# Four places for a feed-forward set's first raw quarters, three for other raw weights, and a 4 KB scratch for GpSimd's transfers

## The chip, the core and the metric

The program runs on one core of a Trainium2 chip: TensorE (PE) multiplies, VectorE (DVE), ScalarE (ACT) and GpSimd (POOL) work element by element, SyncE (SP) and GpSimd issue the transfers from device memory. The metric is device microseconds of one execution, from its first to its last instruction and what lies around it; less is better.

## What is computed

Two layers of an encoder trunk over 768 tokens (512 and 256, two groups that share all weights), in float32. Cut to what matters here:

```python
x = x + W_o( g_att * P_att(DiffAttn(n)) + g_rec * P_rec(BiRGLRU(n)) )   # n = RMSNorm(x)
...
h2 = rmsnorm(x, norm2_g)
return x + jnp.square(jax.nn.relu(h2 @ w_ff1)) @ w_ff2      # D_MODEL 1024, D_FF 4096
```

The change touches how the weights of all these products are brought in, above all those of the last line.

## The kernel before

**Precision and products.** Every float32 operand is split into a rounded part `hi` and a remainder `lo`; a product takes three matmuls (hi·hi, hi·lo, lo·hi).

**Feed-forward.** The 4096 hidden columns are worked in 8 pieces of 512 (loop over `c`). A piece has a first stage (`w_ff1`, lines 1028 to 1030) and a second (`w_ff2`, lines 1099 to 1102). Each is a 2x2 block product by Strassen's scheme: 7 products in place of 8, from 4 raw quarters `a1`, `b1`, `b2`, `a2` of the weight block and from sums of them. One set of weights is thus 4 loads of 128x1024 floats and 7 operands: `a1`, `a2`, `b2` as they are, `P1 = b1 + b2`, `P2 = P1 ± a1`, `P3 = a1 ± b1` (written over `b1`), `P4 = a2 ± P2` (written over `P2`). The four sums are DVE instructions of line 250. The second stage takes its products in the order 1, 2, 6, 5, 3, 7, 4 (`FP2`), 24 matmuls each. After each half of a product DVE adds the accumulator into the residual `x` (line 1069, tiles sY or sZ), and the next product may write that accumulator only after this. DVE also forms sums of the hidden blocks (line 1069, tiles e) and their `lo` parts (line 213, tiles sZ or sX; in the first layer sZ): the operands `o2[q]` of the products.

**Weights.** `prefetch` walks a fixed list (`plan`) and prepares up to 8 operands ahead. A sum, and every weight that is no raw quarter, is split by ACT (line 210, `whi`) and DVE (line 213, `wlo`). A raw quarter `a1`, `a2`, `b2` is rounded and negated by ACT (lines 294, 295), and a transfer that GpSimd issues (line 296) adds the raw quarter from device memory into `wlo`. `whi` and `wlo` have 4 places each (`WB`).

**Places.** `a1` and `b1` of a set lie in tiles `rw` with 2 places, `b2` and `a2` in tiles `raw` with 2 places, which all other raw weights use too. SP issues these loads in the order of the program; a load waits until the place it takes is free, and those behind it wait with it.

**Order.** TensorE's order is written by hand. On the other engines a scheduler orders the program by its own estimate of when operands are ready; each engine then works strictly in that order.

Of the kernel before, what the change touches and what calls it, by code (L numbers as in the profile page):

```python
# [9 lines left out]
F32 = mybir.dt.float32  # L10
# [6 lines left out]
P = 128  # L17
# [66 lines left out]
def trunk_kernel(ctx: ExitStack, tc: tile.TileContext, xT, wqk, wv, wx, wy, wg0, wg1, wa, wr, wo, wf1, wf2,  # L84
                 wf2s, rgw, vec, rep, rot, out):
    nc = tc.nc
# [3 lines left out]
    wp = ctx.enter_context(tc.tile_pool(name="wp", bufs=1))  # L90
# [112 lines left out]
    def nm(s):  # L203
        uid[0] += 1
        return f"{s}_{uid[0]}"

    def split(hi, lo, src, eng="act"):

        if eng == "act":
            S.activation(hi, src, AF.Copy)  # L210
        else:
            V.tensor_copy(out=hi, in_=src)
        V.tensor_tensor(out=lo, in0=src, in1=hi.bitcast(F32), op=ALU.subtract)  # L213
# [29 lines left out]
    fw, fpool = {}, [None]  # L243

    def ff_operand(w, l, c, x):

        ep_, sub = fpool[0], w == "wf2"

        def two(out, u, v, op):
            V.tensor_tensor(out=fw[out], in0=fw[u], in1=fw[v], op=op)  # L250

        if x == "a1":
            for i, y in enumerate(("a1", "b1", "b2", "a2")):
                if i < 2:
                    fw[y] = ep_.tile([P, 1024], F32, tag="rw", name=nm("rw"), bufs=2)
                else:
                    fw[y] = wp.tile([P, 1024], F32, tag="raw", name=nm("raw"), bufs=2)
                fw["d" + y] = WT[w][l][c][i]
                nc.sync.dma_start(out=fw[y], in_=fw["d" + y])
            fw["P1"] = fw["P2"] = None  # L260
        if x in ("P1", "P2") and fw["P1"] is None:
            fw["P1"] = ep_.tile([P, 1024], F32, tag="ws", name=nm("ws"), bufs=2)
            two("P1", "b1", "b2", ALU.add)
        if x == "P2":
            fw[x] = ep_.tile([P, 1024], F32, tag="ws", name=nm("ws"), bufs=2)
            two(x, "P1", "a1", ALU.subtract if sub else ALU.add)
        elif x == "P3":
            fw[x] = fw["b1"]
            two(x, "a1", "b1", ALU.subtract if sub else ALU.add)
        elif x == "P4":  # L270
            fw[x] = fw["P2"]
            two(x, "a2", "P2", ALU.subtract if sub else ALU.add)
        return fw[x], fw.get("d" + x)

    def prefetch(upto):
        while len(ready) < min(upto, len(plan)):
            k = plan[len(ready)]
            acc = None
            if k[0] in ("wf1", "wf2"):
                (raw, acc), n = ff_operand(*k), 1024  # L280
            else:
                src = WT[k[0]]
                for x in k[1:]:
                    src = src[x]
                n = src.shape[1]
                raw = wp.tile([P, n], F32, tag="raw", name=nm("raw"), bufs=2)
                nc.sync.dma_start(out=raw, in_=src)
            hi = wp.tile([P, n], F32R, tag="whi", name=nm("whi"), bufs=WB)
            lo = wp.tile([P, n], F32R, tag="wlo", name=nm("wlo"), bufs=WB)
            if acc is None:  # L290
                split(hi, lo, raw)
            else:

                S.activation(hi, raw, AF.Copy)  # L294
                S.activation(lo, hi.bitcast(F32), AF.Copy, scale=-1.0)  # L295
                G.dma_start(out=lo, in_=acc, accum_op=ALU.add)  # L296
            ready.append((hi, lo))

    def wload(*key):
        i = pos[0]  # L300
        pos[0] += 1
        assert plan[i] == key, (plan[i], key)
        prefetch(i + 1 + AHEAD)
        r, ready[i] = ready[i], None
        return r
# [115 lines left out]
    def norm1(l, xt, alloc):  # L421

        nh = [slot(gh, F32R) for k in range(KT)]
        nl = [slot(gl, F32R) for k in range(KT)]
        ss, st_ = [], []

        def sums():
            if not st_:
                st_.append(slots(gx, F32R))
            return st_[0]  # L430

        for g in range(2):
            if g:
                prefetch(4)
            ss.append(squares(xt, g, alloc, sums, lambda k: prep(xt, vt[l][:, V_N1:V_N1 + KT], nh, nl, g, k)))
        return nh, nl, ss
# [6 lines left out]
    for k in range(KT):  # L443
        if k % 4 == 0:
            prefetch(1 + k // 4)
        nc.sync.dma_start(out=xt[k][:, 0:TA], in_=xT[k][:, 0:TA])
# [7 lines left out]
    for l in range(DEPTH):  # L454
# [292 lines left out]
        def chain():  # L747
            for kind, i in FILL:
                yield from (vproj(i, rtok) if kind == "wv" else proj(i, rtok) if kind == "wqk" else gate0(rb))

        n, it = 0, chain()
# [24 lines left out]
        for j in range(KT):  # L776
# [3 lines left out]
            for g in range(2):  # L780
                off, n = GROUPS[g]
# [134 lines left out]
        for j in range(KT):  # L916
# [5 lines left out]
            for g in range(2):  # L922
                off, n = GROUPS[g]
# [54 lines left out]
        for j in range(KT):  # L978
            w1 = wload("wo", l, j)
            for g in range(2):  # L980
                off, n = GROUPS[g]
# [235 lines left out]
```

## Time and profile before

| | |
|---|---|
| runs shown (3) | 2791.74, 2795.38, 2795.95 us; median 2795.38 |
| profiled execution | 2797.47 us, of which the span is 2795.7 |
| mean granted TensorE clock | 0.976 of full |
| busy | PE 2620.9 us, DVE 1987.8, ACT 1582.9, POOL 175.5 |
| moved by transfers | 248.08 MB, mean 89 GB/s |

The two layers have the same stages: attention, its projection, the recurrent branch, the output product, then the feed-forward, whose pieces follow each other some 71 us apart. A timeline row gives start and length of an instruction; what stands in brackets is how long its engine had stood before it, and which instruction ended that. [...]

### The profile page before, as it was taken

To read this page: it belongs to the slowest core of one execution; us is meant where nothing else is said; L and a number is where in the kernel's file an instruction comes from. 1 tells how busy PE (TensorE), PEld (TensorE's weight loads), DVE (VectorE), ACT (ScalarE), POOL (GpSimd) and SP (SyncE) were. 2 spreads that over 40 slices of the span, in tenths; PEclk is the share of its full clock that TensorE was granted. 3 is DMA by queue.
4 is the path that set the end of the run, shared out by engine and by line. 5 is a ranking of instruction groups with operands and counts; after the bars stand their busy time and mean duration, and the time that the engine had idled before them with its cause. 6 is when DMAs were issued, how large, how long until landed. Compare 5 with 4: busy or idle time off the path is not lost.

```text
span 2795.7 us, 40462 instructions
## 1 busy us (share of the span) xinstructions
PE 2620.9 (94%) x16096; PEld 2458.3 (88%) x16096; DVE 1987.8 (71%) x3243; ACT 1582.9 (57%) x2570; POOL 175.5 (6%) x227
## 2 busy tenths in 40 slices
PE   8999999999998888888899999999999988888889
PEld 8999888888888888888899998888888888888889
DVE  8877863798568666666568788637984686666666
ACT  7787861677235444444467878616772354444444
POOL 0000000000200000000100000000003000000000
PEclk9999999999999999999999999999999999999999
DMA  3111123122424444444321111232224144444444
GB/s 127 59 46 56 50 95 106 60 70 95 136 64 106 106 106 106 106 103 101 104 66 59 48 54 50 94 106 64 65 95 143 58 106 106 106 106 105 106 102 110
DMA packets 70877, 248.08 MB, mean 89 GB/s; under 512 B 8992, under 2 KB 12448, under 8 KB 70688
## 3 DMA queue, kind: packets, MB, share of 16 engines
q1 hardware_dynamic: 48384, 161.50, 17.9%
q0 software_dynamic: 21584, 83.37, 13.7%
q8 instruction: 126, 2.06, 0.3%
q10 hardware_dynamic: 720, 0.62, 0.1%
q14 instruction: 63, 0.52, 0.1%
HBM read 226.59 MB, written 18.87 MB: 88 GB/s over the span
## 4 chain that ended last, share of the span: by engine, by line
PE 54%; DVE 19%; issue 17%; DMA 5%; ACT 4%; POOL 1%; DVEq 0%; ACTq 0%; POOLq 0%
PE d L311 6%; PE d L313 6%; PE d L312 6%; PE d L1028 5%; PE d L1029 5%; PE d L1030 5%; DMA rw<-wf 5%; DVE wlo L213 4%; DVE sZ L1069 2%; DVE sY L1069 2%; PE d L474 2%; PE d L473 2%; PE d L472 2%; PE d L336 2%; PE d L335 2%
## 5 line engine op out<-in xcount | busy, mean ns | idle before, releaser
L210 ACT ACTIVATE whi<-raw 128x1024 fp32r<-128x1024 f32 (+1 forms) x180 | 183.4, 1020 | 320.6 <-PE d L312 162.7
L213 DVE TENSOR_TENSOR wlo<-raw,whi 128x1024 fp32r<-128x1024 f32 (+1 forms) x180 | 218.8, 1219 | 44.9 <-ACT whi L210 43.8
L210 ACT ACTIVATE whi<-ws 128x1024 fp32r<-128x1024 f32 x93 | 98.6, 1060 | 167.5 <-DVE ws L250 105.2
L1099 PE MATMUL d<-sX,whi 128*128 128x384 f32 x448 | 157.3, 351 | 34.3 <-DVE sZ L1069 34.3
L1101 PE MATMUL d<-sX,whi 128*128 128x384 f32 x448 | 157.5, 352 | 32.0 <-DVE sX L213 32.0
L1099 PE MATMUL d<-sZ,whi 128*128 128x384 f32 x392 | 138.3, 353 | 33.1 <-DVE sY L1069 33.1
L1101 PE MATMUL d<-sZ,whi 128*128 128x384 f32 x392 | 138.5, 353 | 31.9 <-DVE sZ L213 31.9
L294 ACT ACTIVATE whi<-raw 128x1024 fp32r<-128x1024 f32 x62 | 65.4, 1055 | 178.9 <-PE d L1101 156.2
L1102 PE MATMUL d<-sX,wlo 128*128 128x384 f32 x448 | 156.2, 349 | 0.0
L311 PE MATMUL d<-sZ,whi 128*128 128x512 f32 (+1 forms) x448 | 150.8, 337 | 0.2 <-DVE rec L403 0.2
L312 PE MATMUL d<-sZ,whi 128*128 128x512 f32 (+1 forms) x448 | 150.8, 337 | 0.0
L312 PE MATMUL d<-sX,whi 128*128 128x512 f32 (+1 forms) x448 | 150.8, 336 | 0.0
L313 PE MATMUL d<-sZ,wlo 128*128 128x512 f32 (+1 forms) x448 | 150.6, 336 | 0.0
L296 POOL DMA_DIRECT2D wlo<-wf x93 | 81.2, 874 | 1098.4 <-ACT wlo L295 1046.1
L472 PE MATMUL d<-whi,sY 128*128 128x256 f32 x512 | 147.8, 289 | 0.0
L472 PE MATMUL d<-whi,sZ 128*128 128x256 f32 x512 | 147.4, 288 | 0.0
L201 ACT ACTIVATE p<-s,nb,sc 128x512 f32<-128x512 f32 (+1 forms) x192 | 134.6, 703 | 21.4 <-DVE nb L652 19.7
L474 PE MATMUL d<-whi,sZ 128*128 128x256 f32 x512 | 145.3, 284 | 0.0
L473 PE MATMUL d<-wlo,sY 128*128 128x256 f32 x512 | 145.2, 283 | 0.0
L474 PE MATMUL d<-whi,sX 128*128 128x256 f32 x512 | 144.7, 283 | 0.0
L473 PE MATMUL d<-wlo,sZ 128*128 128x256 f32 x512 | 144.7, 283 | 0.0
L213 DVE TENSOR_TENSOR wlo<-ws,whi 128x1024 fp32r<-128x1024 f32 x93 | 113.4, 1219 | 43.4 <-ACT whi L210 43.3
(388 smaller groups left out, 9093.6 us busy)
## 6 DMA issues: line engine op xcount, KB each, us to landing
wlo<-wf POOLq DMA_DIRECT2D x93, 512.0 KB, 6.9
rw<-wf SPq DMA_DIRECT2D x62, 512.0 KB, 3.9
raw<-wf SPq DMA_DIRECT2D x62, 512.0 KB, 3.6
raw<-wqk SPq DMA_DIRECT2D x32, 512.0 KB, 4.0
raw<-wg SPq DMA_DIRECT2D x32, 512.0 KB, 3.7
raw<-wv SPq DMA_DIRECT2D x16, 512.0 KB, 3.9
raw<-wa SPq DMA_DIRECT2D x16, 512.0 KB, 4.2
raw<-wx SPq DMA_DIRECT2D x16, 512.0 KB, 3.7
```

What stands on the lines that cost most here:

```text
L210: S.activation(hi, src, AF.Copy)
L213: V.tensor_tensor(out=lo, in0=src, in1=hi.bitcast(F32), op=ALU.subtract)
L311: PE.matmul(ps, lhsT=wh, rhs=xh, start=(k == 0), stop=False)
L312: PE.matmul(ps, lhsT=wh, rhs=xl, start=False, stop=False)
L313: PE.matmul(ps, lhsT=wl, rhs=xh, start=False, stop=(k == n - 1))
L472: PE.matmul(j, lhsT=xh, rhs=hi[:, kk], start=(k == 0), stop=False)
L473: PE.matmul(j, lhsT=xh, rhs=lo[:, kk], start=False, stop=False)
L474: PE.matmul(j, lhsT=xl, rhs=hi[:, kk], start=False, stop=(k == 7))
L1028: PE.matmul(ps, lhsT=hi[:, k], rhs=oh, start=new and k == 0, stop=False, skip_group_check=True)
L1099: PE.matmul(ps, lhsT=hi[:, r, k], rhs=oh[:, k], start=q in (1, 2, 7) and k == 0, stop=False, skip_group_check=True)
L1101: PE.matmul(ps, lhsT=hi[:, r, k], rhs=ol[:, k], start=False, stop=False, skip_group_check=True)
L1102: PE.matmul(ps, lhsT=lo[:, r, k], rhs=oh[:, k], start=False, stop=k == 1, skip_group_check=True)
```

## The change

Three numbers: `rw` gets 4 places, `raw` gets 3, and the part of SBUF that is set aside for the transfers issued by GpSimd shrinks from the default (16384 bytes a partition in the built program) to 4096. Three tiles of 4096 bytes take up what that sets free.

```diff
@@ -252,9 +252,9 @@
         if x == "a1":
             for i, y in enumerate(("a1", "b1", "b2", "a2")):
                 if i < 2:
-                    fw[y] = ep_.tile([P, 1024], F32, tag="rw", name=nm("rw"), bufs=2)
+                    fw[y] = ep_.tile([P, 1024], F32, tag="rw", name=nm("rw"), bufs=4)
                 else:
-                    fw[y] = wp.tile([P, 1024], F32, tag="raw", name=nm("raw"), bufs=2)
+                    fw[y] = wp.tile([P, 1024], F32, tag="raw", name=nm("raw"), bufs=3)
@@ -283,7 +283,7 @@
-                raw = wp.tile([P, n], F32, tag="raw", name=nm("raw"), bufs=2)
+                raw = wp.tile([P, n], F32, tag="raw", name=nm("raw"), bufs=3)
                 nc.sync.dma_start(out=raw, in_=src)
@@ -1202,7 +1202,7 @@
-    nc = _bacc.Bacc("TRN2", target_bir_lowering=False, num_devices=1)
+    nc = _bacc.Bacc("TRN2", target_bir_lowering=False, num_devices=1, dynamic_dma_scratch_size=4096)
```

TensorE's and GpSimd's rows are the same in both programs; those of DVE, ACT and SP move. Three places, all in the second stage of piece 2 of the first layer (1010 to 1052 us in the trace of before). In the names, rw_1757, rw_1758, raw_1759 and raw_1760 are a1, b1, b2, a2 of the next set (first stage of piece 3), ws_1767 is its P1 and ws_1774 its P2, later its P4; rw_1791, rw_1792, raw_1793 and ws_1806 are a1, b1, b2 and P1 of the set after that. sY are the residual, sZ_1781 and sZ_1784 the `lo` parts for products 7 and 4.

DVE, from the middle of product 5's additions to product 4's operand, before:

```order
L1069 TENSOR_TENSOR sY_1516_8698<-sY_1516_8698,d_1771_10656 128x2x384
L1069 TENSOR_TENSOR e_1735_10370<-e_1735_10370,e_1732_10367 128x768
L1069 TENSOR_TENSOR sY_1513_8695<-sY_1513_8695,d_1770_10642 128x2x384
L250 TENSOR_TENSOR ws_1767_10636<-rw_1758_10567,raw_1759_10569 128x1024
L1069 TENSOR_TENSOR sY_1515_8697<-sY_1515_8697,d_1771_10656 128x2x384
L250 TENSOR_TENSOR ws_1774_10677<-ws_1767_10636,rw_1757_10565 128x1024
L1069 TENSOR_TENSOR sY_1514_8696<-sY_1514_8696,d_1789_10816 128x2x384
L213 TENSOR_TENSOR wlo_1769_10639<-ws_1767_10636,whi_1768_10638 128x1024
L1069 TENSOR_TENSOR sY_1516_8698<-sY_1516_8698,d_1790_10830 128x2x384
L213 TENSOR_TENSOR wlo_1776_10680<-ws_1774_10677,whi_1775_10679 128x1024
L250 TENSOR_TENSOR rw_1758_10567<-rw_1757_10565,rw_1758_10567 128x1024
L213 TENSOR_TENSOR sZ_1784_10777<-e_1735_10370,sZ_1784_10777 128x768
```

DVE, the same stretch now (product 5's first addition stands just ahead; sZ_1784 is the next row after the last):

```order
L250 TENSOR_TENSOR ws_1767_10636<-rw_1758_10567,raw_1759_10569 128x1024
L1069 TENSOR_TENSOR sY_1516_8698<-sY_1516_8698,d_1771_10656 128x2x384
L250 TENSOR_TENSOR ws_1774_10677<-ws_1767_10636,rw_1757_10565 128x1024
L1069 TENSOR_TENSOR sY_1513_8695<-sY_1513_8695,d_1770_10642 128x2x384
L213 TENSOR_TENSOR sZ_1781_10742<-e_1733_10368,sZ_1781_10742 128x768
L1069 TENSOR_TENSOR sY_1515_8697<-sY_1515_8697,d_1771_10656 128x2x384
L213 TENSOR_TENSOR wlo_1769_10639<-ws_1767_10636,whi_1768_10638 128x1024
L1069 TENSOR_TENSOR e_1735_10370<-e_1735_10370,e_1732_10367 128x768
L1069 TENSOR_TENSOR sY_1514_8696<-sY_1514_8696,d_1789_10816 128x2x384
L250 TENSOR_TENSOR rw_1758_10567<-rw_1757_10565,rw_1758_10567 128x1024
L1069 TENSOR_TENSOR sY_1516_8698<-sY_1516_8698,d_1790_10830 128x2x384
L213 TENSOR_TENSOR wlo_1776_10680<-ws_1774_10677,whi_1775_10679 128x1024
```

Between product 5's first addition and sZ_1784 the same instructions stand in both; the sum ws_1767 has moved ahead of four of them.

DVE, from sZ_1784 to the next first stage, now (before, the two rows that write ws_1806 and rw_1792 stood behind wlo_1786):

```order
L213 TENSOR_TENSOR sZ_1784_10777<-e_1735_10370,sZ_1784_10777 128x768
L250 TENSOR_TENSOR ws_1774_10677<-raw_1760_10571,ws_1774_10677 128x1024
L250 TENSOR_TENSOR ws_1806_10924<-rw_1792_10846,raw_1793_10848 128x1024
L250 TENSOR_TENSOR rw_1792_10846<-rw_1791_10844,rw_1792_10846 128x1024
L1069 TENSOR_TENSOR sY_1514_8696<-sY_1514_8696,d_1789_10816 128x2x384
L1069 TENSOR_TENSOR sY_1516_8698<-sY_1516_8698,d_1790_10830 128x2x384
L213 TENSOR_TENSOR wlo_1783_10748<-rw_1758_10567,whi_1782_10747 128x1024
L213 TENSOR_TENSOR wlo_1786_10782<-ws_1774_10677,whi_1785_10781 128x1024
L250 TENSOR_TENSOR ws_1807_10926<-ws_1806_10924,rw_1791_10844 128x1024
```

Two sums of the set after next now stand ahead of the additions of product 4.

SP, the loads of these sets, now:

```order
L259 DMA rw_1757_10565<-wf1 128x1024
L259 DMA raw_1729_10333<-wf2 128x1024
L259 DMA rw_1758_10567<-wf1 128x1024
L259 DMA raw_1759_10569<-wf1 128x1024
L259 DMA rw_1791_10844<-wf2 128x1024
L259 DMA raw_1760_10571<-wf1 128x1024
L259 DMA raw_1793_10848<-wf2 128x1024
L259 DMA rw_1792_10846<-wf2 128x1024
```

Before, SP issued raw_1729 ahead of rw_1757, then raw_1759, raw_1760, rw_1758, rw_1791, raw_1793, rw_1792: rw_1758 came last of its set. In the built programs rw_1758 takes the place of rw_1727 (P3 of the set in use, read last by wlo_1753) before, and that of the same quarter of the set two before (first stage of piece 2) now; raw_1759 takes the place of raw_1729 before, and that of b2 of the set two before now; raw_1793 now takes that of raw_1728, and rw_1792 that of rw_1727.

## Rows read from the trace of the kernel before

**Rows 1.** Windows: us, busy PE, PEld, DVE, ACT, POOL, granted clock, DMA share, GB/s.

```profile
600.00:800.00 200.00, 199.45 (x1141) 175.13 (x1141) 136.41 (x193) 103.73 (x131) 24.99 (x24) 1.00 0.31 103
...
796.90:868.00 71.10, 71.10 (x413) 66.03 (x412) 55.71 (x87) 43.92 (x70) 4.39 (x5) 1.00 0.35 83
...
1010.10:1081.20 71.10, 61.76 (x338) 60.93 (x337) 48.04 (x56) 32.61 (x41) 5.24 (x6) 0.93 0.45 104
```

**Rows 2.** Waits of PE: total us, times, longest.

```profile
PE d L1099 <- DVE sZ L1069: 34.3, 15, 4.0
PE d L1099 <- DVE sY L1069: 33.1, 14, 3.9
PE d L1101 <- DVE sX L213: 32.0, 7, 4.6
PE d L1101 <- DVE sZ L213: 31.9, 7, 4.6
```

**Rows 3.** Timeline of PE, second stage of piece 2, first layer.

```profile
1010.06 0.33 PE L1099 MATMUL d<-sZ,whi 128*128 128x384 f32 x1
...
1040.15 0.41 PE L1099 MATMUL d<-sZ,whi 128*128 128x384 f32 x1 [3.66 <-DVE sY L1069]
1045.20 0.69 PE L1101 MATMUL d<-sZ,whi 128*128 128x384 f32 x1 [4.64 <-DVE sZ L213]
...
1052.07 0.33 PE L1028 MATMUL d<-sX,whi 128*128 128x384 f32 x1
```

**Rows 4.** Timeline of DVE in the same stage.

```profile
1025.52 1.22 DVE L213 TENSOR_TENSOR wlo<-rw,whi 128x1024 fp32r<-128x1024 f32 x1
1026.65 0.95 DVE L1069 TENSOR_TENSOR sY<-sY,d 128x768 f32<-128x768 f32 x1
1027.52 0.95 DVE L213 TENSOR_TENSOR sZ<-e,sZ 128x768 fp32r<-128x768 f32 x1
...
1030.29 0.95 DVE L1069 TENSOR_TENSOR sY<-sY,d 128x768 f32<-128x768 f32 x1
1035.92 1.23 DVE L250 TENSOR_TENSOR ws<-rw,raw 128x1024 f32<-128x1024 f32 x1 [4.68 <-DMA rw<-wf]
...
1044.20 0.95 DVE L213 TENSOR_TENSOR sZ<-e,sZ 128x768 fp32r<-128x768 f32 x1
```

**Rows 5.** Timeline of SP's issues (two in a row are merged).

```profile
1021.93 3.28 SPq L259 DMA_DIRECT2D raw<-wf  x2
1026.76 17.91 SPq L259 DMA_DIRECT2D rw<-wf  x2
```

**Rows 6.** The chain that ended last, 1020 to 1046 us: start, us, what.

```profile
1026.76 9.07 DMA rw<-wf
```

**Rows 7.** Waits of DVE: total us, times, longest.

```profile
DVE ws L250 <- DMA rw<-wf: 69.2, 23, 5.1
```

**Rows 8.** Windows of PE alone: us, busy, granted clock, DMA share, GB/s.

```profile
1036.49:1039.99 3.50, 0.00 (x1) 1.00 0.05 9
...
2645.36:2648.86 3.50, 0.00 (x0) 0.98 0.07 14
...
903.99:913.99 10.00, 9.28 (x45) 0.80 0.29 102
...
2724.00:2734.00 10.00, 9.35 (x38) 0.67 0.19 57
```

**Rows 9.** Timeline of GpSimd.

```profile
703.70 4.30 POOL L937 DMA_DIRECT2D sY<-xT  x8 [10.35 <-PE d L313]
...
1067.25 0.87 POOL L296 DMA_DIRECT2D wlo<-wf  x1 [11.84 <-ACT wlo L295]
...
1077.30 0.88 POOL L296 DMA_DIRECT2D wlo<-wf  x1 [2.96 <-PE d L1030]
```

**Rows 10.** The page's part 6: KB each, median us from issue to landing.

```profile
wlo<-wf POOLq DMA_DIRECT2D x93, 512.0 KB, 6.9
...
sY<-xT POOLq DMA_DIRECT2D x8, 384.0 KB, 6.8
```

## The prediction

> **What bounds the kernel now.** I went from the windows over whole stages to the waits of TensorE (PE), then into one place on three timelines.
>
> The windows [rows 1] show where PE stands. Between 600 and 800 us it is busy 199.45 of 200 us, and in the last stretch before the feed-forward pieces settle (796.90 to 868.00) all of 71.10. In piece 2 of the first layer, 1010.10 to 1081.20, it is busy 61.76 of 71.10 at a mean granted clock of 0.93. So what can be won lies in the pieces, some 9 us of standing in each and what the lower clock takes, and nearly nothing in the stretch from 600 to 800 us.
>
> The waits of PE [rows 2] give the causes. Line 1099 waits for DVE's additions into the residual (15 + 14 times), line 1101 for a `lo` part that DVE writes (7 + 7 times, up to 4.6 us): 131 us in all, mostly at 14 places, one per piece that has another feed-forward set behind it.
>
> One place on PE's timeline [rows 3]: the second stage begins at 1010.06. Product 7 ends at 1040.15 - 3.66 = 1036.49. Product 4 gets one matmul off at 1040.15 and then stands 4.64 us more for its `lo` part. The next first stage begins at 1052.07.
>
> DVE in the same time [rows 4] is dense up to 1031.24 (1030.29 + 0.95). There it stands 4.68 us, and what ends that is a transfer: the sum P1 of the *next* set lacks its raw quarter. The additions and the `lo` part that PE wants stand behind this sum. The last of them starts at 1044.20, and PE goes on at 1045.20. SP's timeline [rows 5] shows why the quarter is late: it was issued at 1026.76, just after DVE had finished reading (1025.52 + 1.22) the old P3 that held its place. The chain [rows 6] gives it 9.07 us to land. DVE's waits [rows 7] show the pattern over the kernel: 69.2 us, longest 5.1; its 23 times include short ones, so I take 4.68 for each of the 14 places (66 us).
>
> **The change part by part.**
>
> *Places.* rw_1758, the late quarter, no longer takes the place of the P3 in use but that of a set two before, and raw_1759 likewise. Both then are free long before 1010, and their loads go out in the first stage. SP's line does not hold them: ahead of them now stand rw_1757 and raw_1729, whose places come free in the same first stage or sooner. So DVE's 4.68 us go. What is late next I find by walking DVE's new order with the pitch of the rows: 1.13 us for 1024 columns (1025.52 to 1026.65), 0.87 for 768 (1026.65 to 1027.52) [rows 4]. From product 5's first addition to sZ_1784 both programs hold the same 14 instructions, nine of 768 and five of 1024 columns: 9 x 0.87 + 5 x 1.13 = 13.5 us. From 1026.65 that ends at 1040.1; before it was 1044.20 + 0.87 = 1045.1. **PE resumes product 4 some 4.9 us earlier, x 14 = 69 us.**
>
> Does something hold DVE on that walk? A product is 24 matmuls of 0.172 us (413 in 71.10 us [rows 1]), 4.1 us. Product 3 ends near 1032.3 and its second addition has its turn at 1032.4; product 7 ends at 1036.5 to 1036.8 and its second addition has its turn at 1037.3. Product 7's `lo` part, moved behind two sums, is ready at 1032.4, some 0.2 us after PE wants it, which product 4's longer wait swallows. PE is then still left standing from about 1036.7 to 1040.2, 3.5 us. DVE stays the bound of this stage, and the rest of its queue is the next to be late.
>
> *Sums moved ahead of product 4's additions.* ws_1806 and rw_1792 have their turn at 1041.3. Their loads take places freed at 1024 to 1026.7, as SP's issues now at 1021.93 to 1026.76 [rows 5]; with the landing of 9.07 us seen here [rows 6] they are there at 1036, so 5 us of cover. They push product 4's second half addition to about 1045.6. The new first stage starts near 1044.3 on an accumulator that the first half addition frees at 1044.4: 0.1 us, taken as nothing. If the cover were gone, each us later than 1041.3 would be a us of PE.
>
> *The first stage* keeps its spacing: the same operands come free and are needed at the same distances, and DVE has three sums less just ahead of its end. I take nothing.
>
> *The clock.* [...] In the 10 us from just before PE resumes, the granted clock is 0.66 to 0.81 at the 14 places (the first and the last of them in [rows 8]); the sum of what is missing is 38 us, of which about 14 x 0.36 (0.7 us at half the clock each) is time in which PE stood: 33 us. How much comes back? In the first 3.50 us of standing the clock read 1.00 in 13 of 14 places and 0.98 in one [rows 8], and the stand left over is 3.5 us. So mostly it would not fall; but it was falling in one, and may fall as PE resumes. I take three quarters: **25 us**. The ends are 0 and 33.
>
> *Third `raw` place elsewhere, DVE and ACT rows moved in the projection stages.* PE stands 0.55 us in 200 there [rows 1]: nothing to win, and loads only come sooner.
>
> *The scratch of 4 KB.* No row shows its filling. From below nothing: in before, 8 transfers were issued within 4.30 us [rows 9] while one takes 6.8 us to land [rows 10], so several lie in it at once, and a smaller one can only delay. From above, if it held one transfer at a time, the price is in the rivals. I take nothing, since GpSimd's issues in the pieces are 3.8 us apart and more (2.96 + 0.87 [rows 9]), so that hardly more than two are under way. [...]
>
> **Sum.** 69 + 25 = 94 us off the profiled execution's 2797.47: 2703.4. That execution lies 2.1 us above the median of the runs shown, so for a median I say **2701**.
>
> **The rivals.**
>
> *The clock falls all the same.* For: a place where it had begun to within 3.50 us. Against: the other 13. 2795.4 - 69 = 2726.
>
> *The loads stay late.* SP works in order; were one of the loads ahead of rw_1758 held until the second stage, DVE would stand as before: 2795, no change. Against: the places they take.
>
> *Scratch for one transfer at a time.* The second of two accumulating loads, issued 2.96 + 0.87 = 3.8 us after the one ahead [rows 9], would land 6.9 - 3.8 = 3.1 us later [rows 10]. It is wanted one product into the next second stage, at 1081.2 + 4.1 = 1085.3, and now lands at 1084.2: 2 us late, x 15 = 30. The burst of 8 would take 54 us in place of 11 [rows 9, 10], which could cost 0 to 43 us a layer, say half. 2701 + 30 + 43 = 2774. Against: 8 issues in 4.30 us show more than one at once before, but with four times the space.
>
> *The scratch slows every accumulating load* (the slower side). The tightest is b2 of a first stage: issued at 1067.25 [rows 9], landed at 1074.2, wanted at 1052.07 + 132 x 0.172 = 1074.8 [rows 1, 3]: 0.6 us of cover. Three times the landing, 20.7 us, would put 13.2 us on each of 15 pieces: 2701 + 198 = 2899. It turns the forecast's gain into a loss from a landing of about 6.9 + 0.6 + 94 / 15 = 13.8 us on. For: the space is a quarter. Against: nothing in before waits for space.
>
> **How the numbers follow.** Forecast 0.72, clock falls 0.13, loads late 0.05, one at a time 0.06, slowed loads 0.04. The low end is all of the clock back, 2693, less the spread of the runs shown (4 us): 2689. The high end is no clock back with 4.68 us a place, 2795.4 - 66 = 2730, plus that spread and a little for the 0.1 to 0.2 us taken as nothing at each place: 2736. The other rivals, 0.15, stay outside. A measurement tells about 0.2%, 6 us, from no change: faster 0.91, same 0.05, slower 0.04.
>
> **What would show it.** In the pieces DVE's wait of line 250 for `rw` must be gone; line 1101 must wait some 3.4 us in place of 4.6, line 1099 no longer 3.6 just ahead of it; a piece must be near 64.4 us long in place of 71.1 (94 / 14 = 6.7 less), and the clock mostly 1.00 after the stand. I am wrong if DVE still stands for a transfer, if PE has new waits on `wlo` from line 296, or if GpSimd's issues last longer than 0.9 us.

## The result, and the profile after

| | before | changed |
|---|---|---|
| median (4 runs each) | 2795.66 us | 2719.85 us |
| lowest to highest | 2791.74 to 2796.11 | 2718.05 to 2720.78 |
| profiled execution, span | 2797.47, 2795.7 | 2719.59, 2717.8 |
| mean granted TensorE clock | 0.976 | 0.99 |

The ratio is 0.9731, with a 95% interval of 0.9714 to 0.9748: 2.7% faster. The forecast of 2701 was 19 us too low, the range of 2689 to 2736 held. Of the 94 us forecast, 78 came (2797.47 - 2719.59 between the two profiled executions).

The waits of PE after (total us, times, longest), against [rows 2]:

```profile
PE d L1101 <- DVE sX L213: 23.4, 7, 3.4
PE d L1101 <- DVE sZ L213: 23.3, 7, 3.4
PE d L1099 <- DVE sZ L1069: 8.3, 8, 1.0
...
PE d L1099 <- DVE sY L1069: 7.3, 7, 1.0
```

Line 1099 has lost its long waits: 15 of 1.0 us are left of 15 + 14. Line 1101 waits 3.3 us in place of 4.6, at the same 14 places. Together 62.3 us in place of 131.3: 69.0 us of standing are gone.

Piece 2 of the first layer, as a window (columns as in [rows 1]), and PE's timeline in its second stage, against [rows 3]:

```profile
999.30:1064.32 65.02, 60.65 (x337) 59.72 (x337) 48.02 (x56) 32.62 (x42) 5.27 (x6) 0.97 0.49 113
```

```profile
1012.81 0.41 PE L1099 MATMUL d<-sZ,whi 128*128 128x384 f32 x1 [1.04 <-DVE sY L1069]
1029.37 0.44 PE L1101 MATMUL d<-sZ,whi 128*128 128x384 f32 x1 [3.33 <-DVE sZ L213]
...
1035.03 0.33 PE L1028 MATMUL d<-sX,whi 128*128 128x384 f32 x1
```

The piece is 65.0 us long in place of 71.1. Its only long stand is the one ahead of product 4.

DVE in that stage, against [rows 4]:

```profile
1014.59 1.21 DVE L213 TENSOR_TENSOR wlo<-rw,whi 128x1024 fp32r<-128x1024 f32 x1
1015.72 0.94 DVE L1069 TENSOR_TENSOR sY<-sY,d 128x768 f32<-128x768 f32 x1
1016.59 1.21 DVE L250 TENSOR_TENSOR ws<-rw,raw 128x1024 f32<-128x1024 f32 x1
1017.72 0.94 DVE L1069 TENSOR_TENSOR sY<-sY,d 128x768 f32<-128x768 f32 x1
...
1027.23 1.22 DVE L213 TENSOR_TENSOR wlo<-ws,whi 128x1024 fp32r<-128x1024 f32 x1
1028.37 0.95 DVE L213 TENSOR_TENSOR sZ<-e,sZ 128x768 fp32r<-128x768 f32 x1
...
1030.37 1.22 DVE L250 TENSOR_TENSOR ws<-rw,raw 128x1024 f32<-128x1024 f32 x1
```

The sum of the next set (1016.59) starts without a gap, and no wait of line 250 is left in DVE's list of waits; before, that was 69.2 us [rows 7]. From product 5's first addition (1015.72) to the end of sZ_1784 (1028.37 + 0.87) are 13.5 us. DVE is dense here: it is now the bound of the stage.

SP's issues, against [rows 5]:

```profile
976.54 0.33 SPq L259 DMA_DIRECT2D rw<-wf  x1
983.60 0.33 SPq L259 DMA_DIRECT2D raw<-wf  x1
990.05 0.33 SPq L259 DMA_DIRECT2D rw<-wf  x1
1011.00 3.28 SPq L259 DMA_DIRECT2D raw<-wf  x2
1015.83 11.01 SPq L259 DMA_DIRECT2D rw<-wf  x2
```

By the order of SP's rows, the issue at 976.54 is rw_1758, the quarter that was late, 40 us ahead of its use; 983.60 is raw_1759, and 1015.83 is rw_1792, 14 us ahead of the sum at 1030.37.

Last, the clock. PE alone (us, busy with the number of matmuls, granted clock as a share of full, DMA share, GB/s): the stand ahead of product 4, the four us behind it, and ten us from just before PE resumes:

```profile
1026.03:1029.37 3.34, 0.01 (x1) 1.00 0.47 156
...
1029.37:1030.37 1.00, 1.00 (x4) 0.72 0.08 33
1030.37:1031.37 1.00, 1.00 (x4) 0.50 0.00 0
1031.37:1032.37 1.00, 1.00 (x4) 0.50 0.00 0
1032.37:1033.37 1.00, 1.00 (x5) 0.58 0.00 0
...
1028.67:1038.67 10.00, 9.30 (x44) 0.83 0.19 67
```

While PE stands, the clock reads 1.00 here, and 0.95 to 1.00 over the 14 stands. It falls to 0.50 about when PE resumes and stays there for some 3.4 us: in the four us behind the stand 0.28 + 0.50 + 0.50 + 0.42 = 1.7 us are missing, which is 3.4 us at half of full. The ten-us window reads 0.83 at all 14 places, so 1.7 us are lost at each, 24 in all, against 33 before ([rows 8] and the prediction's working). That is 9 us back, and 69 + 9 = 78 is the difference that was measured; as the 33 is an estimate, the sum is good to a few us only.

### The profile page after: what moved, and what is told of

Its sections match the earlier page's. It is cut to its first block, busy times and chain, and to the rows that moved or that the text cites. A ratio compares the mean times of both kernels' runs of the same rounds, so it can differ in the third digit from the quotient of the medians.

```text
span 2717.8 us, 40476 instructions
## 1 busy us (share of the span) xinstructions
PE 2612.0 (96%) x16096; PEld 2448.3 (90%) x16096; DVE 1980.8 (73%) x3243; ACT 1583.3 (58%) x2570; POOL 175.4 (6%) x227
## 4 chain that ended last, share of the span: by engine, by line
PE 61%; DVE 21%; issue 11%; ACT 5%; DMA 1%; POOL 0%; DVEq 0%; ACTq 0%; POOLq 0%
PE d L311 7%; PE d L313 6%; PE d L312 6%; PE d L1028 5%; PE d L1029 5%; PE d L1030 5%; DVE wlo L213 4%; PE d L473 3%; PE d L472 3%; PE d L474 3%; DVE sZ L1069 3%; DVE sY L1069 2%; PE s L649 2%; DVE e L1069 2%; PE d L336 2%
## 5 line engine op out<-in xcount | busy, mean ns | idle before, releaser
L210 ACT ACTIVATE whi<-raw 128x1024 fp32r<-128x1024 f32 (+1 forms) x180 | 183.4, 1020 | 317.4 <-PE d L312 175.8
```

## The experiments

The theory: only b1's place mattered; what is left is DVE's order, and the clock that falls behind the stand. Each run was timed against the kernel before on the same chip (medians 2793.4, 2793.8 and 2795.4 in the three groups); its ratio is to that median, with a 95% interval in brackets.

**Four places for `rw` alone.**

```diff
-rw bufs=2, raw bufs=2, default scratch
+rw bufs=4, raw bufs=2, scratch 8192
```

> Four places for rw, two for raw (as before), scratch 8192. Theory (the late quarter is b1, and its place is all that matters): DVE no longer stands for rw, PE's L1101 wait is about 3.3 us at 14 places as with the whole change, and the time is within 4 us of the whole change's 2719.9. Rival (the third raw place is needed too): P1 of the next set then waits for its b2, which takes the place of the a2 in use; DVE stands up to the 4.7 us of before, and the time lies between 2720 and 2795, at 14 us for each us of that stand.

Measured 2719.70 us, ratio 0.9733 (0.9717 to 0.9749); line 1101 waits 23.2 us at 7 places of a layer, 3.3 each, and DVE has no wait for `rw`. The theory holds: the third `raw` place adds nothing to the time that can be measured. DVE does stand for a load in this run, but not where the rival had it:

```profile
DVE ws L250 <- DMA raw<-wf: 47.2, 13, 3.7
```

```profile
1040.22 1.23 DVE L250 TENSOR_TENSOR ws<-rw,raw 128x1024 f32<-128x1024 f32 x1 [3.59 <-DMA raw<-wf]
```

This sum is P1 of the set after next (ws_1806 in the names above), and in this run it stands behind product 4's additions (1033.41 and 1035.68). PE's waits are those of the whole change, so this stand of DVE costs nothing; the third `raw` place takes it away.

**Three places for `raw` alone.**

```diff
-rw bufs=2, raw bufs=2, default scratch
+rw bufs=2, raw bufs=3, scratch 12288
```

> Three places for raw, two for rw (as before), scratch 12288. Theory: b1 is as late as before, DVE stands 4.7 us for rw at 14 places, and the time is within 6 us of 2795.7. Rival (the third raw place brings part of the gain, by moving other loads ahead of b1 on SP or out of its way): faster than before by more than 6 us, at 14 us for each us that DVE's stand is shorter.

Measured 2792.44 us, ratio 0.9993 (0.9983 to 1.0003). DVE's wait in this run, against [rows 7]:

```profile
DVE ws L250 <- DMA rw<-wf: 63.9, 21, 4.9
```

The wait is still there, and the time is that of before.

**The small scratch alone.**

```diff
-nc = _bacc.Bacc("TRN2", target_bir_lowering=False, num_devices=1)
+nc = _bacc.Bacc("TRN2", target_bir_lowering=False, num_devices=1, dynamic_dma_scratch_size=4096)
```

> Places as before (two and two), scratch 4096 alone. Theory: nothing waits for the scratch, the time is within 6 us of 2795.7, and the 8 loads of the residual are issued within 4.3 us as before. Rival (the smaller scratch holds transfers back, and the change's gain would be larger without it): slower than before; one transfer at a time would lengthen that burst from 4.3 us to some 50 and put some 2 us on each piece, 2825 to 2870.

Measured 2795.07 us, ratio 1.0003 (0.9994 to 1.0013). The 8 loads of the residual went out within 4.31 us, as before. The scratch costs nothing that can be measured.

**The whole change with a scratch of 1024.**

```diff
-dynamic_dma_scratch_size=4096
+dynamic_dma_scratch_size=1024
```

> The whole change, but a scratch of 1024. Theory: in the pieces no more than two of GpSimd's transfers are under way at once, so they go as with 4096 and the time stays within 6 us of 2719.9; at most the burst of 8 loads takes longer than 4.3 us, which nothing waits for within 30 us. Rival (the scratch is close to binding): GpSimd's issues in the pieces take longer than the 0.87 us of before, b2 of a first stage, which has 0.6 us of cover, is late, and each us of that costs 15 us.

Measured 2718.51 us, ratio 0.9729 (0.9715 to 0.9744). GpSimd's issues of the residual in this run, against the 8 within 4.30 us of [rows 9]:

```profile
702.73 4.08 POOL L937 DMA_DIRECT2D sY<-xT  x7 [10.34 <-PE d L313]
707.55 0.55 POOL L937 DMA_DIRECT2D sY<-xT  x1 [0.74 <-issue]
```

Seven went out as before, the eighth after a pause of 0.74 us. In the second layer's burst it was seven too, and the eighth 0.63 us later. That the space was full then is my estimate from these two bursts and is not shown: the profile names nothing that GpSimd waited for. The time does not move.

**Three places for `rw`.**

```diff
-rw bufs=2, raw bufs=2, default scratch
+rw bufs=3, raw bufs=2, scratch 12288
```

> Three places for rw, two for raw, scratch 12288. b1 of the next set then takes the place of a1 of the set in use, which is free before the second stage begins, in place of that of the P3 in use. Theory (only this matters): as the whole change, within 4 us of 2719.9, no wait of DVE for rw. Rival (the fourth place keeps later loads out of each other's way): DVE stands for a load again, 14 us of time for each us of it.

Measured 2719.89 us, ratio 0.9734 (0.9718 to 0.9751), with 3.3 us at line 1101 as in the whole change. One more place is enough: b1 then takes that of a1 of the set in use. DVE stands for `raw` as with four places alone (47.2 us, 13 times), and again the time does not show it.

**The whole change, and DVE's urgent rows first.** The operands of products 7 and 4 get a higher priority:

```diff
                     elif q == 5:
-                        o2[7] = h_split(b12)
-                        two(b21, b21, b11, ALU.subtract)
+                        with tc.high_priority(offset=120):
+                            o2[7] = h_split(b12)
+                            two(b21, b21, b11, ALU.subtract)
                     elif q == 3:
-                        o2[4] = h_split(b21)
+                        with tc.high_priority(offset=120):
+                            o2[4] = h_split(b21)
```

> The whole change, and the operands of products 7 and 4 get a higher priority for the scheduler (120 places), so that DVE writes sZ_1784 ahead of the next set's sums. Theory (DVE's order is what PE still waits for, and the clock falls only because PE stands 3.3 us): L1101 no longer waits, the clock stays at 1.00, a piece is 65.0 - 3.3 - 1.7 = 60.0 us and the time 2720 - 14 x 5.0 = 2650. Rival 1 (the clock falls without the stand too): 2720 - 14 x 3.3 = 2673. Rival 2 (the sums, now later, are late for the next first stage): L1028 or L1030 wait instead and less than half of the 70 us comes.

Measured 2643.33 us, ratio 0.9460 (0.9446 to 0.9474): 5.4% under before; with the last run below it is the fastest of the study. A piece of it as a window, two of PE's waits, and DVE around sZ_1784 (at 1011.98):

```profile
989.10:1048.63 59.53, 58.49 (x338) 58.20 (x337) 48.12 (x56) 32.70 (x42) 5.28 (x6) 1.00 0.53 123
```

```profile
PE d L1101 <- DVE sZ L1069: 8.3, 8, 1.0
...
PE d L1101 <- DVE sY L1069: 7.3, 7, 1.0
```

```profile
1009.90 1.22 DVE L250 TENSOR_TENSOR ws<-rw,raw 128x1024 f32<-128x1024 f32 x1
1011.10 0.95 DVE L1069 TENSOR_TENSOR sY<-sY,d 128x768 f32<-128x768 f32 x1
1011.98 0.95 DVE L213 TENSOR_TENSOR sZ<-e,sZ 128x768 fp32r<-128x768 f32 x1
1013.18 0.95 DVE L1069 TENSOR_TENSOR sY<-sY,d 128x768 f32<-128x768 f32 x1 [0.26 <-PE d L1104]
```

(Line 1101 of this program is line 1099 of the change.) Only the 1.04 us ahead of product 5 is left; the clock is 1.00 over the whole piece, PE busy 58.49 of 59.53 us. The theory's 60.0 us a piece was 0.5 too long. PE's timeline of the change shows where that lies: its stand of 3.33 us parts two starts by 3.66 us (1025.71 to 1029.37) that otherwise lie 0.17 apart, which is 3.49 lost, and two starts of product 7's matmuls lose some 0.3 us more (1021.24 to 1021.87). With the priority both are gone. DVE now has gaps in this stage: it waits for PE.

**The same priority on the kernel before.**

```diff
-rw bufs=4, raw bufs=3, scratch 4096 (with the priority)
+rw bufs=2, raw bufs=2, default scratch (with the priority)
```

> The kernel before (two and two places, default scratch) with the same higher priority as in the run on the whole change. DVE's rows of the second stage are then the same as there as far as P2's lo part, and only the places differ. Theory (in this order too the late b1 holds DVE, ahead of product 3's second addition): DVE stands some 4 us for rw, PE some 3.8 us inside product 7, the clock falls; a piece is 6 to 7.8 us shorter than 71.1, the time 2686 to 2711. Rival (with the urgent rows first the place no longer matters): the time of the run with both, near 2650.

Measured 2712.22 us, ratio 0.9706 (0.9692 to 0.9721), 1 us over the range expected. DVE's wait and PE's waits (now at the additions, lines as in the run ahead):

```profile
DVE ws L250 <- DMA rw<-wf: 70.4, 21, 5.0
```

```profile
PE d L1101 <- DVE sZ L1069: 32.1, 15, 3.7
PE d L1101 <- DVE sY L1069: 30.2, 14, 3.7
```

DVE stands as long as in the kernel before, but with less that PE wants queued behind the sum. With the places this becomes 2643.3, so there they are worth 69 us, as in the old order (76): the two do not replace each other.

**A lower priority.** 80 in place of 120 on the whole change.

```diff
-with tc.high_priority(offset=120):
+with tc.high_priority(offset=80):
```

> As the run with the higher priority on the whole change, but 80 places: sZ_1784 then stands behind one sum and one lo part fewer than in the change, and by the walk is ready 2.0 us sooner, so PE stands about 1.9 us in place of 3.3. Theory (a stand of 1.9 us leaves the clock alone): 2720 - 14 x (2.05 + 1.66) = 2668. Rival (it falls after any stand of that kind): 2720 - 14 x 2.05 = 2691.

Measured 2675.71 us, ratio 0.9576 (0.9561 to 0.9590). The wait ahead of product 4 (line 1103 here) in the first layer, and the ten us from just before PE resumes (columns as above), at the first place of the first layer and at the fourth of the second:

```profile
PE d L1103 <- DVE sZ L213: 12.2, 7, 1.7
```

```profile
896.90:906.90 10.00, 9.30 (x53) 1.00 0.44 118
...
2418.68:2428.68 10.00, 9.30 (x44) 0.83 0.31 98
```

The stand is 1.74 us at all 14 places. The clock stays at 1.00 behind 13 of them and falls behind one, the place shown from the second layer. Forecast were 2668 by this theory and 2691 by the rival: the rows are for the theory on the clock at 13 places, but not at every one. Two things make up about the 8 us between the theory's time and the measured one. The stand became 1.59 us shorter (3.33 to 1.74) where 2.05 was reckoned, 6.4 us over 14 places; and the one fall put 1.6 us on its piece (63.1 us to the next place, 61.6 elsewhere in the layer). Smaller differences beside these I have not traced.

The run of the priority on the kernel before has unequal stands, and shows both cases in one program. The same windows there, behind stands of 2.43, 3.24 and, in the second layer, 3.19 us:

```profile
962.78:972.78 10.00, 9.30 (x54) 1.00 0.22 61
1025.84:1035.84 10.00, 9.30 (x45) 0.83 0.15 52
...
2642.34:2652.34 10.00, 9.30 (x54) 1.00 0.26 63
```

Of the 14 places of both layers the clock fell behind 12, with stands of 2.96 to 3.70 us, and held behind two, of 2.43 and 3.19 us. Since it fell behind 2.96 and 3.18 and held behind 3.19, the length of the stand alone does not decide it; what else does, these runs do not show.

**The priority with three `rw` places.**

```diff
-rw bufs=4, raw bufs=3, scratch 4096 (with the priority)
+rw bufs=3, raw bufs=2, scratch 12288 (with the priority)
```

> The higher priority (120 places) with three places for rw, two for raw, scratch 12288. Theory (of the places only that of b1 ever mattered, in this order too): as the run with the whole change and the same priority, within 5 us of 2643.3, and no wait of DVE for rw. Rival (with the shorter piece the loads follow each other more closely and the third raw place or the fourth rw place is needed): DVE stands for a load, and the time is later by 14 us for each us that reaches PE.

Measured 2643.10 us, ratio 0.9459 (0.9443 to 0.9475): as with four and three places. DVE has no wait for `rw`. It does stand for `raw` (32.8 us, 13 times), but nothing of that reaches PE: the rival's stand came, its price did not. In the faster order, too, one place more for `rw` is all that the time needs.

## Why the prediction was right, and where it was off

*The cause.* Right, and shown by undoing and by doing parts alone: places for `rw` alone give the whole gain, for `raw` alone none, the scratch alone none. The places also made the scheduler move DVE's rows, and no run parts the two; that the move by itself gives product 4 nothing is argued, not shown: the same 14 rows run up to sZ_1784 in both orders.

*The size of the stand.* "PE resumes product 4 some 4.9 us earlier, x 14 = 69 us": the waits fell by 69.0 us. The walk along DVE's new order, 13.5 us for 14 instructions, came out at 13.5 us, and the stand left over at 3.3 us where 3.5 was worked out. Product 7's `lo` part came late by about the 0.2 us worked out (two starts of that product lost some 0.3).

*The clock.* This term was mis-sized: "I take three quarters: 25 us". 9 us came. I had taken from [rows 8] that a stand of 3.5 us mostly leaves the clock alone, because it read 1.00 in the first 3.50 us of 13 of 14 stands. The rows of after show what that overlooked: the clock reads 0.95 to 1.00 during the stand, and falls about as PE goes to work again (from 0.4 us before to 0.8 us after), at all 14 places. The step that failed is reading the clock only in the first 3.50 us, while the engine stood; in the kernel before the standing went on, so those rows could not show what follows a short stand. The trace of before had a warning. After its first stand PE does one matmul and stands again, and in this second stand the clock fell (columns as in [rows 8]):

```profile
1040.56:1045.20 4.64, 0.00 (x2) 0.55 0.00 0
```

It reads 0.50 to 0.63 there at all 14 places, so at every one it fell soon after the 3.50 us that I looked at. Where PE goes on, from 1045.00 to 1051.00, it reads 0.50. Of the prediction's signs, "the clock mostly 1.00 after the stand" failed at all 14 places, and a piece is 65.0 us long, not 64.4.

The rival "the clock falls all the same" (2726) was nearer in this, though a shorter time at the lower level (1.7 us lost in place of 33 / 14 = 2.4) put the result between the two.

*What was costed at nothing.* The scratch and the third `raw` place change nothing in the time, by the runs of each alone (ratios 1.0003 and 0.9993). How many transfers 4096 bytes hold at once, no run shows; the eight of a burst went out without a pause with them (4.31 us, against 4.30 before). The moved rows of the projection stages had no run of their own; between 600 and 800 us PE is busy 199.48 of 200 us, 199.45 before [rows 1]. The sums moved ahead of product 4's additions (ws_1806) started without a wait. Neither the rivals of the scratch nor that of late loads came about; the accumulating loads kept their landing (6.6 us after, 6.9 before [rows 10]).

*What bounds the stage now.* "DVE stays the bound of this stage" is shown by the priority, as far as DVE's order goes: the same work on DVE (48.02 us busy in a piece of the change, 48.12 with the priority) in another order takes away the stand and, with it, the clock's fall, 76.5 us more. The amount of DVE's work is not what holds PE.

## What to carry to other kernels

On an engine that works strictly in order, as DVE does here, a load that is late for a *later* step holds up the rows of this step queued behind it (DVE stood 4.68 us for the next set's quarter, and PE 4.64 us for the `lo` part queued behind that sum); look for what stands behind the waiting instruction, and whose place the late load takes. One more place at the right tile was worth as much time as three here (2719.89 and 2719.85 us), so undo each part before paying for all. When a stand is shortened, look at the granted clock in the microseconds after the engine resumes, not only while it stands: here 1.6 us less of standing made a piece 3.45 us shorter at 13 of 14 places.

## What the runs showed of the hardware

In the run of the change the granted clock read 0.95 to 1.00 over stands of 3.3 us, fell between about 0.4 us before and 0.8 us after PE resumed, and stayed at 0.50 of full for some 3.4 us, nearly all of them full work (1.00 us busy in each us behind the stand), at 14 of 14 places. Behind stands of 1.74 us it held at 13 of 14 places and fell at one. In the run with unequal stands it fell behind 12 (2.96 to 3.70 us) and held behind two (2.43 and 3.19 us).

With 1024 bytes a partition of scratch, seven of GpSimd's transfers went out without a pause in both bursts of eight, and the eighth 0.74 and 0.63 us later; with 4096 and with the default all eight of the first layer's burst went out in one go (4.31 and 4.30 us).
